# A strided slice by DMA alone: hand-set semaphores in a critical section against waits set by the tile framework

## The chip, the cores and the metric

The kernel runs on one core of one Trainium2 chip. The metric is the device time of one execution in microseconds; the time of a kernel is the median over its runs. The kernel does no arithmetic: every byte is moved by the core's 16 DMA engines, and the only engines of the core that take part are SyncE (SP) and ScalarE (ACT), both merely as issuers of transfers. A "transfer" below is one `dma_start`.

## What is computed

```
batch, seq, dim = 32, 1024, 512          # x is float32
start, stop, stride = 0, 512, 2
def reference(x, start, stop, stride):
    return x[:, start:stop:stride, :].astype(np.float32)
```

The output has 32 batches of 256 rows of 512 float32, so each row is 2 KB, a batch 512 KB and the whole output 16.78 MB. In the input the rows that are taken stand 4 KB apart (every second row of the first half of each batch).

## The kernel before

The 256 rows of a batch are dealt out by parity into two halves of 128 rows. `two(t, b, step, parity)` picks one half of two batches, b and b + step, as 128 x 2 x 512 elements (512 KB); `apart(b)` says which parity of batch b goes which way.

One half of each batch is copied straight from the input to the output in DRAM (line 41): 16 transfers of 512 KB, two batches each, issued by ACT on its own DMA queue (q10 in the profile). They are called the copies here, copy 0 to copy 15.

The other half goes through SBUF. It is loaded into the tile `held` (128 partitions x 32 batches x 512 elements) by 16 transfers of 512 KB, two batches each (line 40, the loads, load 0 to load 15), and stored to the output by 32 transfers of 256 KB, one batch each (line 46, the stores, store 0 to store 31). Loads and stores are both issued by SP on one queue (q1 in the profile), all loads first.

The order is written out by hand inside one critical section (line 33), in which the framework sets no waits. Each group of eight batches has a semaphore `loaded` that its four loads count up by 16 each; SP waits for the full count of a group (line 43) before it issues that group's eight stores. So SP's instruction stream has four waits among its 48 transfers, and ACT's has none among its 16. At the end SP waits for all stores and all copies (lines 47 and 48). Entering and leaving the critical section costs a small handshake between SP and ACT.

An issuer does not wait for a transfer to be done; it goes on as soon as the transfer is handed over. Where an issue takes several us in the profile, the handing over itself was held up.

Of the kernel before, what the change touches and what calls it, by code (L numbers as in the profile page):

```python
# [3 lines left out]

EIGHT = 8


def apart(b):


    return 1 - (b >> 1 & 1)


def two(t, b, step, parity):

    return t[b : b + step + 1 : step].rearrange("b (p two) d -> two p b d", two=2)[parity]


def kernel(tc, x, start, stop, stride, out):

    nc = tc.nc
    src = x[:, start:stop:stride, :]
    B, rows, D = out.shape
    P = rows // 2
    sp, act = nc.sync, nc.scalar
    groups = range(0, B, EIGHT)  # L30
    with tc.tile_pool(name="io", bufs=1) as io:
        held = io.tile([P, B, D], x.dtype, name="held")
        with tc.tile_critical():
            loaded = [nc.alloc_semaphore(name=f"loaded{g}") for g in groups]
            done = [nc.alloc_semaphore(name=f"done{i}") for i in range(2)]
            for g in groups:
                for i, (b, step) in enumerate(((0, 5), (2, 5), (1, 3), (3, 3))):
                    b += g
                    at = g + 2 * i
                    sp.dma_start(held[:, at : at + 2], two(src, at, 1, 1 - apart(at))).then_inc(loaded[g // EIGHT], 16)  # L40
                    act.dma_start(two(out, b, step, apart(b)), two(src, b, step, apart(b))).then_inc(done[1], 16)
            for g in groups:
                sp.wait_ge(loaded[g // EIGHT], 16 * 4)
                for b in range(g, g + EIGHT):
                    to = out[b].rearrange("(p two) d -> two p d", two=2)[1 - apart(b)]
                    sp.dma_start(to, held[:, b]).then_inc(done[0], 16)
            sp.wait_ge(done[0], 16 * B)
            sp.wait_ge(done[1], 16 * (B // 2))


# [1 line left out]
_INS = ['x', 'start', 'stop', 'stride']  # L52
_OUTS = [((32, 256, 512), 'float32')]

_NUMBERS = {'start': 0, 'stop': 512, 'stride': 2}


def kernel(**inputs):
    import numpy as _np
    import concourse.bacc as _bacc  # L60
    import concourse.tile as _tile
    from concourse import mybir as _mybir
    from concourse.bass_utils import run_bass_kernel_spmd as _run

    nc = _bacc.Bacc("TRN2", target_bir_lowering=False, num_devices=1)  # L65
    arrays, args = {}, []
    for name in _INS:
        if name in _NUMBERS:
            args.append(_NUMBERS[name])
            continue  # L70
        a = _np.ascontiguousarray(inputs[name])
        if a.dtype.kind in "iu":
            a = a.astype(_np.int64)
        arrays[f"in_{name}_dram"] = a
        args.append(nc.dram_tensor(f"in_{name}_dram", a.shape, _mybir.dt.from_np(a.dtype), kind="ExternalInput").ap())
    for i, (shape, dtype) in enumerate(_OUTS):
        dt = _mybir.dt.from_np(_np.dtype(dtype))
        args.append(nc.dram_tensor(f"out_{i}_dram", shape, dt, kind="ExternalOutput").ap())
    with _tile.TileContext(nc) as tc:
        kernel(tc, *args)  # L80
    r = _run(nc, [arrays], core_ids=[0])
    got = tuple(r.results[0][f"out_{i}_dram"] for i in range(len(_OUTS)))
    return got[0]
```

## Time and profile before

| | |
|---|---|
| median of 7 runs | 81.12 us (80.43 to 81.68) |
| the profiled execution's own time | 81.0 us |
| its span, first to last instruction | 79.2 us |
| time around the span | 1.8 us |
| loads: issue, duration of one (min / median / max) | 437 / 1556 / 7242 ns |
| copies: the same | 662 / 1863 / 5182 ns |
| stores: the same | 492 / 642 / 4267 ns |
| first issue of a load, first and last issue of a store | 0.9 us, 34.0 us, 67.4 us |

The page has a row for each compute engine that is busy (here only POOL, with four tiny fills of constants at the start), then a digit per fortieth of the span for how busy the 16 DMA engines were, and the rate in GB/s that they moved. A transfer is counted once in the moved bytes, so the 25.17 MB are 8.39 MB of loads, 8.39 MB of copies and 8.39 MB of stores. Issues of transfers are not counted as busy time of an engine; they have a section of their own, with the time from an issue to the landing of its last byte. A DMA share slightly above 1 means that packets of one engine overlap a little in the record.

A landing can also be read from the semaphores: each transfer adds 16, one from each DMA engine, and the time of the sixteenth is its landing. Where many transfers share a semaphore, the records are taken in sixteens in order of time.

### The profile page before, as it was taken

How to read it: one execution, taken by the hardware profiler on the slowest of the kernel's cores; microseconds unless marked ns; L12 is line 12 of the kernel's file. 1: busy time of each engine (PE TensorE's matmuls, PEld its weight loads, DVE VectorE, ACT ScalarE, POOL GpSimd, SP SyncE). 2: the span in 40 equal slices, each digit the busy share in tenths (PEclk: the TensorE clock that was granted, in tenths of full speed). 3: DMA queues.
4: the chain of work that ended last, by engine and by line, in shares of the span. 5: the costliest groups of instructions: out<-in, count | busy, mean ns of one | idle time of the engine just before them, and what ended most of it. 6: DMA issues, size and time to landing. Idle time of an engine off the chain costs nothing. (4 is left out here: it accounts for less than half of the span.)

```text
span 79.2 us, 115 instructions
## 1 busy us (share of the span) xinstructions
POOL 0.2 (0%) x4
## 2 busy tenths in 40 slices
POOL 1000000000000000000000000000000000000000
DMA  0899989999999999999999999999999999999970
GB/s 0 251 310 239 331 281 329 342 344 358 320 341 379 344 337 269 261 332 316 349 344 357 374 279 347 344 291 404 408 404 383 351 342 362 349 360 359 350 260 7
DMA packets 13312, 25.17 MB, mean 318 GB/s; under 512 B 1024, under 2 KB 1024, under 8 KB 13312
## 3 DMA queue, kind: packets, MB, share of 16 engines
q1 hardware_dynamic: 8960, 16.78, 64.9%
q10 hardware_dynamic: 4352, 8.39, 30.6%
HBM read 16.78 MB, written 16.78 MB: 424 GB/s over the span
## 5 line engine op out<-in xcount | busy, mean ns | idle before, releaser
L65 POOL MEMSET const-bfloat16-1.0<- 128x1 bf16 x1 | 0.1, 101 | 0.0
L65 POOL MEMSET const-uint8-127<- 128x1 uint8 x1 | 0.1, 101 | 0.0
L65 POOL MEMSET const-float32-0.0<- 128x1 f32 x1 | 0.1, 98 | 0.2 <-issue 0.2
L65 POOL MEMSET const-float32-1.0<- 128x1 f32 x1 | 0.1, 98 | 0.0
## 6 DMA issues: line engine op xcount, KB each, us to landing
out_dram<-in_x_dram ACTq DMA_DIRECT2D x16, 512.0 KB, 22.3
held<-in_x_dram SPq DMA_DIRECT2D x16, 512.0 KB, 22.4
out_dram<-held SPq DMA_DIRECT2D x32, 256.0 KB, 10.3
```

What stands on the lines that cost most here:

```text
L65: nc = _bacc.Bacc("TRN2", target_bir_lowering=False, num_devices=1)
```

## The change

The critical section, its hand-made semaphores and the waits on them go. `held` becomes 16 tiles, one per load. The same loads, copies and stores are written in the same order on the same two queues, and the tile framework places the waits.

```
-    groups = range(0, B, EIGHT)
     with tc.tile_pool(name="io", bufs=1) as io:
-        held = io.tile([P, B, D], x.dtype, name="held")
-        with tc.tile_critical():
-            loaded = [nc.alloc_semaphore(name=f"loaded{g}") for g in groups]
-            done = [nc.alloc_semaphore(name=f"done{i}") for i in range(2)]
-            for g in groups:
-                for i, (b, step) in enumerate(((0, 5), (2, 5), (1, 3), (3, 3))):
-                    b += g
-                    at = g + 2 * i
-                    sp.dma_start(held[:, at : at + 2], two(src, at, 1, 1 - apart(at))).then_inc(loaded[g // EIGHT], 16)
-                    act.dma_start(two(out, b, step, apart(b)), two(src, b, step, apart(b))).then_inc(done[1], 16)
-            for g in groups:
-                sp.wait_ge(loaded[g // EIGHT], 16 * 4)
-                for b in range(g, g + EIGHT):
-                    to = out[b].rearrange("(p two) d -> two p d", two=2)[1 - apart(b)]
-                    sp.dma_start(to, held[:, b]).then_inc(done[0], 16)
-            sp.wait_ge(done[0], 16 * B)
-            sp.wait_ge(done[1], 16 * (B // 2))
+        held = [io.tile([P, 2, D], x.dtype, name=f"held{i}") for i in range(B // 2)]
+        for g in range(0, B, EIGHT):
+            for i, (b, step) in enumerate(((0, 5), (2, 5), (1, 3), (3, 3))):
+                b += g
+                at = g + 2 * i
+                sp.dma_start(held[at // 2], two(src, at, 1, 1 - apart(at)))
+                act.dma_start(two(out, b, step, apart(b)), two(src, b, step, apart(b)))
+        for b in range(B):
+            to = out[b].rearrange("(p two) d -> two p d", two=2)[1 - apart(b)]
+            sp.dma_start(to, held[b // 2][:, b % 2])
```

In the built program of the changed kernel the framework uses eight DMA semaphores, `DMAHW0` to `DMAHW7`, and deals them out in turn in the order of the program: copies get the even ones, loads the odd ones, and the stores go through all eight. Every transfer waits until the transfer before it on its semaphore has landed in full. A cut of the listing, with the count each waits for:

```
ACT copy 0   ->DMAHW0        SP load 0   ->DMAHW1
ACT copy 1   ->DMAHW2        SP load 1   ->DMAHW3
...
ACT copy 4   waits DMAHW0 16     SP load 4   waits DMAHW1 16
...
ACT copy 15  waits DMAHW6 48     SP load 15  waits DMAHW7 48
SP store 0   waits DMAHW0 64     SP store 1   waits DMAHW1 64
...
SP store 31  waits DMAHW7 112
```

So copy i waits for copy i - 4, load i for load i - 4, stores 0, 2, 4 and 6 for copies 12 to 15, stores 1, 3, 5 and 7 for loads 12 to 15, and store j from 8 on for store j - 8. At the end SP waits for all eight semaphores. The number of transfers and of bytes is the same, and so is the order on each queue.

## Prediction

> **What bounds the kernel now.** I read the page first: does anything but the DMA engines matter, and are these ever idle?
>
> ```profile
> span 79.2 us, 115 instructions
> ...
> DMA  0899989999999999999999999999999999999970
> GB/s 0 251 310 239 331 281 329 342 344 358 320 341 379 344 337 269 261 332 316 349 344 357 374 279 347 344 291 404 408 404 383 351 342 362 349 360 359 350 260 7
> ...
> q1 hardware_dynamic: 8960, 16.78, 64.9%
> q10 hardware_dynamic: 4352, 8.39, 30.6%
> ```
>
> The two queues together fill 64.9 + 30.6 = 95.5% of the 16 engines' time over the whole span. Only the first slice and the last two are not near full. The second view is the same by stages, in stretches that I chose from the semaphore landings: both queues run until about 54.5 us (load 15 lands at 54.5, copy 15 at 55.9), stores alone after that.
>
> ```profile
> core 0: us, POOL busy (x), PEclk, DMA share, GB/s
> 0.00:5.00 5.00, 0.20 (x4) 1.00 0.53 171
> 5.00:10.00 5.00, 0.00 (x0) 1.00 0.97 283
> 10.00:12.00 2.00, 0.00 (x0) 1.00 0.82 282
> 12.00:54.50 42.50, 0.00 (x0) 1.00 1.02 333
> 54.50:59.50 5.00, 0.00 (x0) 1.00 1.05 404
> 60.00:75.00 15.00, 0.00 (x0) 1.00 1.06 355
> 75.00:76.00 1.00, 0.00 (x0) 1.00 0.94 315
> 76.00:77.00 1.00, 0.00 (x0) 1.00 0.70 268
> 77.00:78.00 1.00, 0.00 (x0) 1.00 0.09 35
> ```
>
> The columns are length, POOL, clock, DMA share and rate. The engines are full from about 5 us to 75 us, so an issuer matters only if it leaves a queue empty. The third view says how far the issuers run ahead: time from issue to landing, for loads (L40), copies (L41) and stores (L46).
>
> ```profile
> L40 SPq DMA_DIRECT2D held<-in_x_dram x16: 437/1556/7242, 0.9 to 30.7; - x16
> DMA to landing us min/median/max: 4.1/22.4/27.4
> ...
> L41 ACTq DMA_DIRECT2D out_dram<-in_x_dram x16: 662/1863/5182, 0.9 to 33.6; - x16
> DMA to landing us min/median/max: 6.4/22.3/25.3
> ...
> L46 SPq DMA_DIRECT2D out_dram<-held x32: 492/642/4267, 34.0 to 67.4; - x32
> DMA to landing us min/median/max: 9.2/10.3/21.3
> ```
>
> A load takes 4.1 us when nothing lies ahead of it (load 0) and 22.4 us in the median: the difference is waiting in line. Stores are issued from 34.0 us, yet none lands before 53 us, as SP's queue is served in order and the loads are ahead of them. The last view is the end of SP's chain:
>
> ```profile
> SPq L33 <- DMA out_dram<-held: 10.0, 1, 10.0
> ```
>
> SP issues its last store at 67.4 us and then has 10 us with nothing to do but wait. The DMA engines set the end, not SP.
>
> **The change part by part.** No byte, transfer or queue order changes, so the sum starts from the profiled execution's 81.0 us (0.12 under the median of 81.12; span 79.2 and 1.8 around it). What changes is how many transfers may be in flight.
>
> *Loads and copies: at most 4 per queue.* Before, the limit is the queue itself: the issue of load 9 runs from 8.85 to 16.1 us and ends as load 3 lands (16.2 us by the semaphores), so about 6 are in flight. Now load i waits for load i - 4. Four loads and four copies are 8 x 0.524 = 4.19 MB; at the 324 GB/s of this stage (all of 2.0 to 54.5 us) that is 12.9 us of work. A new transfer needs 4.1 us (load 0) to 6.4 us (copy 0) from issue to landing on near-empty queues. When load i - 4 lands, three loads are still queued, 3 x 3.24 us = 9.7 us of work beside the copies, against at most 6.4 us to bring in the next. The engines do not run in step: the first and the last of a load's sixteen increments lie 1.2 to 3.1 us apart. Even an engine 3.1 us ahead has 9.7 - 3.1 = 6.6 us. Cost 0; the cover is the three queued transfers. Behind the waiting instruction stand all later loads and stores on SP and all later copies on ACT. From below: if the dip at 10 to 12 us (share 0.82) comes from the held-up issues, it goes, a gain of 2 x 0.18 = 0.36 us. From above: losing 3% of the stage, about the difference between shares of 1.02 and 0.99, is 1.6 us. I take 0, nearest to the row of 12 to 54.5 us.
>
> *Turn from loads to stores.* Store 0 now waits for copy 12, which landed at 46.7 us, where before SP issued it at 34.0. Behind it on SP stand the 31 other stores. At 46.7 us, loads 13, 14 and 15 (landing at 47.8, 51.1, 54.5) are still on SP's queue, so it has 7.8 us of its own work left. Store 2 follows copy 13 (50.1 us), store 4 copy 14 (53.4), store 6 copy 15 (55.9). So when loads end at 54.5, stores 0 to 5 are queued: 6 x 0.262 MB / 404 GB/s = 3.9 us. Store 6 enters at 55.9 and store 7 half a us later. Cost 0, with 54.5 + 3.9 - 55.9 = 2.5 us to spare, less what stores 0 to 5 were served earlier in the copies' place (which is no loss, as the engines then worked on them).
>
> *Stores: at most 8 in flight,* where the 10.3 us median and 355 GB/s (0.74 us a store) make about 14 before. Eight are 8 x 0.74 = 5.9 us of work. An unqueued round trip is not in the trace; the nearest row is load 0 with 4.1 us, for twice the bytes and a cold start, so it bounds a store's from above, unless engines that lag add to it. They do: at the end the share falls from 0.94 to 0.09 between 75 and 77.6 us, so the fastest engine ends about 2.4 us before the slowest. For the last engine, whose landing releases the next store, seven are still queued (5.2 us) against 4.1 us. It never runs dry. One that leads may, for 4.1 + 2.4 - 5.9 = 0.6 us, which moves no end. SP keeps up: 0.64 us per issue (median) against 0.74 us drained. Cost 0; bounds: +1.8 us (three rounds of eight that each expose 0.6) and -1.0 us (leading engines held back, so that the late engines end sooner: the idle area of 75 to 77.6 us is 0.12 + 0.36 + 0.97 over 1.06, less the 0.4 us after the last packet).
>
> Here a rule stands against the change. The Trainium skill, "DMA: Bandwidth & Descriptors", section "Anatomy of one DMA — SWDGE (gpsimd) path", says that a transfer has a fixed cost near 2.0 us, mostly the receipt of the last byte, and that engines never wait on semaphores, so a wait holds the issuer and all behind it. Read harshly, an estimate by that page, the 32 stores would go in four rounds of eight, each exposing 2.0 us: 8 us more, 89.0. By the row of load 0 against the window of 5.9 us it is 0, because stores are replaced one by one. No run here shows a waited store yet.
>
> *Entry and exit of the section.* In the trace's records SP's entry signal and its wait stand between the start barrier (0.65 us) and the first load (0.94 us); removing them is worth about 0.1 us. At the end SP's wait is over at 78.11 us and its final barrier begins at 78.59 us. Between them lies the handshake with ACT. In its place come four waits for semaphores and a drain, of which two are left once store 31 has landed, at some 0.07 us each (the spacing of SP's records there). So 0.48 - 0.14 = 0.34 us. Both are on the path: -0.44 us. Bounds 0 and -0.6.
>
> Sum: 81.0 + 0 + 0 + 0 - 0.44 = 80.56, rounded to 80.6 us.
>
> **The rivals.**
> *Slower: the window of eight stores is too short.* It decides once a store's round trip, lag of engines included, is over 5.9 us. For: 4.1 + 2.4 = 6.5 us is over it. Against: those 2.4 us are the lead of the first engines and not a delay of the late ones. Price: 3 x (6.5 - 5.9) = 1.8 us, so 81.0 - 0.44 + 1.8 = 82.4. At 7.0 us it would be 3.3 us, 83.9.
> *Slower: the window of four in the first stage.* For: it is a third less than the queue held. Against: the four loads and three copies issued in the first 3 us landed after 9.8 and 11.3 us in the median, so they alone kept the engines busy to about 12 us. Price: 1.6 us, 82.2.
> *Faster: a shorter line serves better.* Engines kept closer together end together (-1.0), or the dip at 10 to 12 us goes (-0.36). For: the ragged end; in 54.5 to 59.5 us the rate is 404, later 355 GB/s, so engines slow each other. Against: the lag of an engine, 3 stores, is less than the window of 8, so it hardly holds them back. 79.6 with the first alone, 79.2 with both.
> *The change does nothing that shows:* waits placed differently, each covered, and the 0.44 us lost in the spread of 80.43 to 81.68. That gives 81.0.
>
> **How the numbers follow.** Covered waits with the shorter entry and exit, 80.6: 0.40. Nothing at all, 81.0: 0.12. Store window 0.18, first window 0.12, faster 0.18. The range leaves out half of the faster case below 79.5 and the store window's worse part above 82.7, together a good 0.15. A difference of 1% (0.8 us) is about what a measurement of this kernel can tell from none. Against the median the likeliest is -0.55%, so some of its chance (0.08) passes the 1% with the faster case: faster 0.26. The two slower windows less a little that stays inside 1%: slower 0.28. Within 1%: 0.46. Cases of both signs hold a part, so the likeliest one's own range is 80.1 to 81.1.
>
> **What would show it.** Median time to landing falls from 22.4 to some 13 us for loads and from 10.3 to some 6 us for stores. The share stays at 1.0 or more from 12 to 75 us. Issues of loads last about 0.5 to 0.9 us, never 7, and their waits appear on SP and ACT instead. The first store is issued at 46 to 47 us and the last at 71 to 73 us. SP's final wait is 5 to 6 us instead of 10. From the last landing to the end it takes 0.8 us instead of 1.1. The prediction is wrong if the share sags below 1 between 56 and 74 us (store window), between 12 and 54 us (first window), or if packets get quicker at the same share, which nothing here accounts for.

## The result, and the profile after

| | before | after |
|---|---|---|
| median | 80.79 us (59 runs) | 80.23 us (24 runs) |
| ratio | | 0.9936, 95% interval 0.9919 to 0.9953 |
| the profiled execution's own time | 81.0 us | 80.27 us |
| its span | 79.2 us | 78.5 us |

With more runs than the prediction had, the kernel before has a median of 80.79 us. By the ratio the change takes 0.64% off it, 0.52 us (0.38 to 0.65). The forecast was 80.6 us from 81.0, that is 0.44 us less. Executions that took over 1.5% longer than the fastest of the same kernel are left out of all ratios and intervals, and of the times of direct_only and raw_mixed below.

The page of the changed kernel, the same rows as were read of the kernel before:

```profile
span 78.5 us, 109 instructions
...
DMA  0898999997999999999999999999999999999990
GB/s 5 291 281 245 303 317 337 325 349 258 361 371 364 310 370 348 314 341 278 310 384 332 363 329 316 346 266 402 406 405 392 350 348 361 351 355 359 354 307 25
...
q1 hardware_dynamic: 8960, 16.78, 64.8%
q10 hardware_dynamic: 4352, 8.39, 31.8%
```

The DMA engines are as full as before: the same bytes on the same queues, 64.8 + 31.8 = 96.6% of a span that is 0.7 us shorter. By stages (length, POOL, clock, DMA share, rate):

```profile
core 0: us, POOL busy (x), PEclk, DMA share, GB/s
0.00:5.00 5.00, 0.20 (x4) 1.00 0.58 178
5.00:10.00 5.00, 0.00 (x0) 1.00 0.88 276
10.00:12.00 2.00, 0.00 (x0) 1.00 0.98 327
12.00:54.50 42.50, 0.00 (x0) 1.00 1.02 334
54.50:59.50 5.00, 0.00 (x0) 1.00 1.05 406
60.00:75.00 15.00, 0.00 (x0) 1.00 1.06 355
75.00:76.00 1.00, 0.00 (x0) 1.00 0.96 324
76.00:77.00 1.00, 0.00 (x0) 1.00 0.46 170
```

From 12 to 75 us share and rate are those of before to within 2 GB/s (333, 404 and 355 then). The whole stage of loads and copies, 2 to 54.5 us, moved 326 GB/s against 324. The dip of 10 to 12 us is gone, but there is one at 5 to 10 us instead. What did change is the length of the lines: time from issue to landing of loads, copies and stores in the changed kernel, and how long one issue takes (ns, min/median/max):

```profile
L36 SPq DMA_DIRECT2D held<-in_x_dram x16: 367/368/844, 0.7 to 41.0; - x16
DMA to landing us min/median/max: 4.2/12.6/14.5
...
L37 ACTq DMA_DIRECT2D out_dram<-in_x_dram x16: 580/580/904, 0.7 to 43.5; - x16
DMA to landing us min/median/max: 6.2/12.6/14.6
...
L40 SPq DMA_DIRECT2D out_dram<-held x32: 332/608/767, 46.4 to 72.2; - x32
DMA to landing us min/median/max: 3.8/5.6/9.1
```

The median load lands after 12.6 us instead of 22.4, the median store after 5.6 instead of 10.3. No issue is held up for several us any more: a load's issue took up to 7242 ns and now at most 844. That time is now spent in waits, which SP's waits show (waiter, what it waited for, us in total, times, longest):

```profile
SPq L36 <- DMA held<-in_x_dram: 33.7, 12, 4.1
SPq L40 <- DMA out_dram<-in_x_dram: 11.5, 4, 5.0
SPq L71 <- DMA out_dram<-held: 5.0, 4, 3.4
SPq L40 <- DMA out_dram<-held: 1.5, 5, 0.4
```

These are 46.7 us of new waits ahead of transfers, and yet the engines are full. Where the 0.7 us of span went is seen at its ends:

```profile
0.73 43.31 ACTq L37 DMA_DIRECT2D out_dram<-in_x_dram  x16
0.73 40.65 SPq L36 DMA_DIRECT2D held<-in_x_dram  x16
46.39 26.14 SPq L40 DMA_DIRECT2D out_dram<-held  x32
```

The first load is issued at 0.73 us instead of 0.94. At the end, from the last landing in the semaphore records to the end of the span, it takes 0.79 us (77.69 to 78.48) instead of 1.16 (78.06 to 79.22). Together 0.20 + 0.37 = 0.57 us. Between first issue and last landing lie 76.96 us against 77.16, a difference of 0.2 us, which is less than this stretch differs from profile to profile (76.35 to 77.65 in crit_windows, raw_no_tile, before_sections4, crit_stores4, raw_short and raw_long_again below, which keep the order of the transfers).

### The profile page after: what moved, and what is told of

Read it like the earlier page. It is cut to its first block, busy times and chain, and to the rows that moved or that the text cites. A ratio compares the mean times of both kernels' runs of the same rounds, so it can differ in the third digit from the quotient of the medians.

```text
span 78.5 us, 109 instructions
## 1 busy us (share of the span) xinstructions
POOL 0.2 (0%) x4
## 3 DMA queue, kind: packets, MB, share of 16 engines
q1 hardware_dynamic: 8960, 16.78, 64.8%
q10 hardware_dynamic: 4352, 8.39, 31.8%
HBM read 16.78 MB, written 16.78 MB: 428 GB/s over the span
## 6 DMA issues: line engine op xcount, KB each, us to landing
out_dram<-in_x_dram ACTq DMA_DIRECT2D x16, 512.0 KB, 12.6
held<-in_x_dram SPq DMA_DIRECT2D x16, 512.0 KB, 12.6
```

## Experiments

Theory A: the gain is the handshakes of the critical section at both ends, and the shorter lines are free because what is still queued covers each wait. Theory B: a shorter line serves better, and the handshakes are hidden. Theory C: the waits cost something, and a larger gain at the ends pays for it. All kernels below write the whole output. The code is cut to the lines that matter, and some of them are shortened.

**crit_windows: the waits alone.**

```
 with tc.tile_critical():
+    # a semaphore for each of 4 loads, 4 copies and 8 stores
     ...
+    if n >= 4: sp.wait_ge(lane[n % 4], 16 * (n // 4))
     sp.dma_start(held[:, at : at + 2], ...).then_inc(lane[n % 4], 16)
+    if n >= 4: act.wait_ge(copied[n % 4], 16 * (n // 4))
     act.dma_start(...).then_inc(copied[n % 4], 16)
     ...
+    if b < 8:  sp.wait_ge((copied, lane)[b % 2][b // 2], 64)
+    if b >= 8: sp.wait_ge(stored[b % 8], 16 * (b // 8))
     sp.dma_start(to, held[:, b]).then_inc(stored[b % 8], 16)
```

> The critical section stays, with its entry and exit, but every transfer waits as in the changed kernel (loads and copies for the one four earlier, stores 0 to 7 for copies and loads 12 to 15, later stores for the one eight earlier). Theory A (the gain is the handshakes at both ends, the shorter lines are free): as before, 80.8 us, ratio 0.998 to 1.002. Theory B (the gain is the shorter line, which serves better, and the handshakes are hidden): as the changed kernel, 80.2 us, ratio 0.992 to 0.995. Theory C (the shorter line costs something that a larger gain at the ends paid for): over 81.0 us, ratio 1.003 or more.

Measured: 80.32 us, before 80.35; ratio 1.0004 (0.9981 to 1.0027). The lines are as short as in the changed kernel, and the first load is issued where it was before; the section on DMA issues (KB each, median us to landing) and the order of time:

```profile
out_dram<-in_x_dram ACTq DMA_DIRECT2D x16, 512.0 KB, 12.4
held<-in_x_dram SPq DMA_DIRECT2D x16, 512.0 KB, 12.0
out_dram<-held SPq DMA_DIRECT2D x32, 256.0 KB, 5.3
```

```profile
0.91 43.37 ACTq L47 DMA_DIRECT2D out_dram<-in_x_dram  x16
0.94 40.40 SPq L44 DMA_DIRECT2D held<-in_x_dram  x16
```

The waits by themselves are worth nothing within 0.2 us either way. Theory B's 0.992 to 0.995 lies outside the interval, C's 1.003 just outside. A stands. The traces of this chip agree: from first issue to last landing it takes 76.37 and 76.43 us with short lines (crit_windows, crit_stores4) and 76.63 and 76.35 us with long ones (raw_no_tile, before_sections4).

**raw_no_tile: the ends alone.**

```
-with tc.tile_pool(name="io", bufs=1) as io:
-    held = io.tile([P, B, D], x.dtype, name="held")
-    with tc.tile_critical():
+held = nc.alloc_sbuf_tensor("held", [P, B, D], x.dtype).ap()
     ...
-with _tile.TileContext(nc) as tc:
-    tile_strided_slice_kernel(tc, *args)
+tile_strided_slice_kernel(nc, *args)
```

> The kernel before with its own four waits and its long lines, but without the critical section and also without the framework's closing barriers. Theory A: 0.2 us less at the entry; at the exit the 1.1 us from the last landing to the end of the span shrink to about 0.1 us, so 1.2 us less in all, 79.6 us, ratio 0.985. Theory B: the line is as long as before, so no gain from it; at most the closing barriers (0.6 us) go, 80.2 us or more, ratio 0.993 to 1.0.

Measured: 78.91 us, ratio 0.9834 (0.9791 to 0.9876). The order of time and the section on DMA issues:

```profile
0.73 33.45 SPq L37 DMA_DIRECT2D held<-in_x_dram  x16
```

```profile
held<-in_x_dram SPq DMA_DIRECT2D x16, 512.0 KB, 21.9
```

Loads land after 21.9 us in the median, so the lines are long. The first load is issued at 0.73 us, and from the last landing to the end there are 0.04 us instead of 1.16. That is 0.20 + 1.12 = 1.32 us of the span. The time around the span is shorter too, 78.77 - 77.4 = 1.4 us instead of 1.8, so 1.7 us go at the ends in all. By the ratio it is 0.0166 x 80.35 = 1.33 us (1.0 to 1.7), and for the same code on another chip (raw_long_again below) 0.0211 x 81.22 = 1.71 us. Within the noise, what goes at the ends goes from the time, one for one.

**before_sections4: the suspected cost, more often.**

```
 with tc.tile_pool(name="io", bufs=1) as io:
     held = io.tile([P, B, D], x.dtype, name="held")
+    for _ in range(4):
+        with tc.tile_critical():
+            sp.nop()
+            act.nop()
     with tc.tile_critical():
```

> The kernel before with four more critical sections ahead of its own, each holding one empty instruction on SP and one on ACT, so that four more entries and exits lie ahead of the first transfer. Theory A: each costs what its entry (0.21 us) and exit (0.35 us) cost at the ends, 4 x 0.55 = 2.2 us more, 83.0 us (82.6 to 83.6), ratio 1.027. Theory B: they are hidden, 80.8 us, ratio 1.00.

Measured: 82.99 us, ratio 1.0338 (1.0306 to 1.0371), 2.7 us more. In order of time:

```profile
3.22 34.88 ACTq L45 DMA_DIRECT2D out_dram<-in_x_dram  x16
3.25 32.50 SPq L44 DMA_DIRECT2D held<-in_x_dram  x16
```

The first load starts 3.25 - 0.94 = 2.31 us later, 0.58 us for each section, where 0.55 was expected. The handshakes are not hidden. The ratio's 2.5 to 3.0 us is somewhat more than these 2.3; where the rest lies is open. That the time itself met the forecast of 83.0 us is luck: the kernel before took 80.35 us on this chip, not the 80.8 that the forecast started from.

**crit_stores4, crit_stores2: how much cover the store window has.** As crit_windows, with four or two stores in flight and no store waiting for a copy.

```
-    if b < 8:  sp.wait_ge((copied, lane)[b % 2][b // 2], 64)
-    if b >= 8: sp.wait_ge(stored[b % 8], 16 * (b // 8))
+    if b % 2 == 0: sp.wait_ge(lane[b // 2 % 4], 16 * (b // 8 + 1))
+    if b >= 4: sp.wait_ge(stored[b % 4], 16 * (b // 4))     # or 2
```

> The kernel before with loads and copies limited to four in flight and stores to four instead of eight; no store waits for a copy. Theory A with a window that must cover a store's round trip: four stores are 4 x 0.74 = 2.95 us of work, the shortest store in the changed kernel's trace takes 3.8 us from issue to landing, so each of 7 rounds of four exposes at least 0.85 us: 6 us more, 86.8 us; with the lag between engines (2.4 us) added to the round trip up to 92 us. Rival (the memory sets the pace of stores at 355 GB/s and the depth of the line does not matter): 80.8 us.

Measured: 80.08 us, ratio 0.9981 (0.9958 to 1.0005). My number for the round trip was wrong. The stores of that run:

```profile
L55 SPq DMA_DIRECT2D out_dram<-held x32: 332/332/709, 42.0 to 74.7; - x32
DMA to landing us min/median/max: 2.3/2.9/13.5
```

The shortest store of the changed kernel (3.8 us) had still waited in line, by 1.5 us or more. Even here the median of 2.9 us is about the work of the four stores in flight (2.95 us), so it can hold time in line too, and the next run had two.

> As the run with four stores in flight, but with two. There a store took 2.9 us from issue to landing in the median and 2.3 us at the least, and four of them (2.95 us of work) just covered it. Two are 1.48 us of work. Theory A2 (a window must cover the round trip of a store that has nothing ahead of it, and that is 2.3 us, not the 3.8 to 4.1 us that I took): a store every 2.3/2 = 1.15 us instead of 0.74, 32 x 0.41 = 13 us more, 93.5 us (90 to 96). Rival (even two keep the memory busy): 80.4 us.

Measured: 91.02 us, ratio 1.1313 (1.1255 to 1.1372). Its page and its stores:

```profile
DMA  0899999999999999999999994666666666666661
GB/s 5 290 278 292 327 273 299 387 379 342 358 372 341 327 267 346 285 366 361 361 350 323 334 343 173 236 236 245 257 253 248 251 239 250 252 251 253 250 242 74
```

```profile
L55 SPq DMA_DIRECT2D out_dram<-held x32: 332/332/591, 41.7 to 85.5; - x32
DMA to landing us min/median/max: 2.1/2.1/13.2
```

This is what a window that is too short looks like: the digits fall to 6 for the whole stage, and 250 GB/s are two stores (0.524 MB) in 2.1 us. A store takes 2.1 us there whether the store before it was issued some 0.6 or 1.5 us earlier, so it does not wait in line, and 2.1 us is its round trip. (In crit_turn_last below, store 0 meets empty queues and takes 2.2 us.) Theory A2 holds with that number, and the time lies in its 90 to 96 us: the window of eight, 5.9 us of work, covers the round trip almost three times.

**crit_loads2: the first window.** As crit_stores4 with two loads, two copies and eight stores in flight.

> The critical section with two loads and two copies in flight instead of four and four; eight stores. Theory A by the rows of the prediction: a pair of transfers needs 4.2 to 6.2 us from issue to landing and engines lie 1.2 to 3.1 us apart, so a round trip near 7.5 us against 6.5 us of work in the window: each of 16 pairs takes 3.75 us instead of 3.24, 8 us more, 88.4 us (84 to 92). Theory A2 (round trips on a short line are shorter than these rows, as with the stores): within 1% of 80.4 us.

Measured: 84.53 us, ratio 1.0503 (1.0438 to 1.0568), at the lower edge of theory A's range: 0.0503 x 80.56 = 4.1 us more where its sum had 8. Copies and loads by the section on DMA issues, and the stretch from 12 to 54.5 us:

```profile
out_dram<-in_x_dram ACTq DMA_DIRECT2D x16, 512.0 KB, 7.4
held<-in_x_dram SPq DMA_DIRECT2D x16, 512.0 KB, 6.7
```

```profile
12.00:54.50 42.50, 0.00 (x0) 1.00 0.99 312
```

A load's landing takes 6.7 us in the median there, a copy's 7.4, against 6.5 us of work in the window. The rate is 312 GB/s where it was 333. So four in flight cover the wait and two do not; three were not tried.

**crit_turn_last: the turn from loads to stores.** As crit_stores4 with eight stores in flight, but store 0 waits for all copies:

```
+    if b == 0:
+        for k in range(4): sp.wait_ge(copied[k], 64)
```

> The critical section with windows of four, four and eight, and store 0 waits for the last copy (about 55.9 us) instead of copy 12 (46.4 us), so SP's queue holds no store when the last load lands. Theory A (the prediction's cover of 2.5 us at the turn is real and its loss is paid in full): the last engines run dry from about 55.5 us until store 0 arrives, some 0.4 us of wait and issue and 1 us to its first packet, so 1.6 us more (1.2 to 2.6), 82.0 us, ratio 1.020. Rival (the stores' stage goes at the memory's 355 GB/s after a first stretch at 405, so a gap at its start is made up by a longer quick stretch): less than 0.5 us more, ratio under 1.006.

Measured: 82.06 us, ratio 1.0193 (1.0144 to 1.0242), theory A's 1.020. The page and SP's longest wait for a copy:

```profile
DMA  0898899999999899899999999945999999999980
GB/s 0 268 290 262 281 340 328 351 331 376 361 323 367 296 288 366 300 333 322 369 342 368 284 342 375 321 163 209 383 377 387 378 358 358 356 356 364 353 294 3
```

```profile
SPq L52 <- DMA out_dram<-in_x_dram: 12.8, 1, 12.8
```

The first store is issued at 54.3 us instead of 46.4, and the two digits 4 and 5, from 52 to 56 us, are the hole. Part of it is made up, as the rival said: from 60 to 75 us the rate is 364 GB/s instead of 355. In the changed kernel the same place has digits of 9: the waits for copies 12 to 15, one by one, keep the queue fed. One more dependence here costs 1.9% (1.4 to 2.4).

**direct_only: can the bound be moved?** Built as the changed kernel, without SBUF:

```
-sp.dma_start(held[at // 2], two(src, at, 1, 1 - apart(at)))
+sp.dma_start(two(out, b, step, 1 - apart(b)), two(src, b, step, 1 - apart(b)))
 act.dma_start(two(out, b, step, apart(b)), two(src, b, step, apart(b)))
-for b in range(B): ...
```

> Built in the manner of the changed kernel, but both halves of every batch go from DRAM to DRAM, 16 copies on each of the two queues, none through SBUF: 8.39 MB fewer pass the DMA engines (8192 packets of 2 KB instead of 12288), while DRAM is read and written as before. Theory A (the DMA engines' packets are the bound, 95 to 97 ns each): 8192/16 x 0.096 = 49 us and 4 us at the ends, 53 us. Rival (DRAM traffic is the bound: in the first stage 326 GB/s moved are 163 of loads and 163 of copies, so 326 read and 163 written, 489 GB/s): 33.55 MB / 489 GB/s = 68.6 us and 4 us, 72.6 us.

Measured: 82.66 us (82.62 and 82.70), ratio 1.0271 (1.0202 to 1.034). Neither was right.

```profile
12.00:54.50 42.50, 0.00 (x0) 1.00 0.94 218
60.00:75.00 15.00, 0.00 (x0) 1.00 0.96 219
```

The engines are nearly full but move 218 GB/s: a third fewer packets of 2 KB, each longer (142 and 137 ns in the mean on the two queues, against 98 and 97 in the changed kernel). A full DMA share is thus no proof that the engines themselves are the bound.

**raw_short, raw_mixed, raw_stores_act, raw_long_again: is there a version that beats both?** All without critical section and closing barriers. The first has four loads, four copies and four stores in flight, the second issues each pair of stores after the load four places on, the third gives the stores to ACT.

```
 raw_mixed:        for i in range(4, 16): load(sp, i); store(sp, i - 4)
 raw_stores_act:   for i in range(16): load(sp, i); copy(sp, i // 2) if i % 2
                   for i in range(16): store(act, i)
                   for i in range(8, 16): copy(sp, i)
```

> As the run without critical section and closing barriers, but with four loads, four copies and four stores in flight. Theory A (the lines' length is free down to these windows; what the ends cost is independent of it): as that run with its long lines, ratio 0.983 (0.980 to 0.987). Rival (a short line gives 0.2% by itself, as the run with four stores hinted, 0.9981 with an interval that reached 1.0005): 0.981 or less, 0.4 us under the other with several runs.

Measured: 79.23 us, ratio 0.9724 (0.9698 to 0.9749). That is below theory A's range and within the rival's "0.981 or less", but further down than the 0.2% that the rival gave to a short line.

> As the run without critical section, but SP issues the stores of a pair of batches after the load four places on, so that loads and stores alternate on its queue, beside ACT's copies and after them. Theory A (the stages stay full whatever the order; the sum of packets sets the time): as without, 79.2 us, ratio 0.983. Rival (stores alone are paced by the memory's writes at 355 GB/s, while mixed with loads the engines go at up to 404): the 8.39 MB of the last stage take 20.8 us instead of 23.6, 2 to 3 us less, 76.5 us, ratio 0.95.

Measured: 82.68 us, ratio 1.0103 (1.0039 to 1.0166). Neither was right. The copies are done at 59.1 us, and from 60 to 75 us, with loads and stores alone on one queue, the rate is 335 GB/s where stores alone had 355; from 12 to 54.5 us it is 322 instead of 333. So the mix did not go faster, which the rival needed; why is open.

> As the run without critical section, but ACT issues the stores from the first load on, and SP issues loads and copies, two loads to a copy and then the last eight copies. Theory A: the order is free, ratio 0.983 or so. Rival (a mix with reads all the time is better than writes alone at the end): 76 to 77 us, ratio 0.95. Against both: DRAM to DRAM copies alone moved 219 GB/s, so if the last eight copies (4.19 MB) run without loads beside them they take 19 us instead of 13 at 326 GB/s, 85 us.

Measured: 85.92 us, ratio 1.0562 (1.0503 to 1.0621), near the 85 us of the warning in its last sentence, but not for its reason. The last eight copies take from 68 to 84 us, and until 77.6 us stores run beside them. After that copies run alone, on one queue, and the page has these slices of 2.1 us for it (the last two full ones, 78.0 to 82.2 us):

```profile
DMA  0998899999989999999999999999999999999992
GB/s 6 315 274 264 272 399 404 272 353 318 267 259 390 359 252 211 307 405 368 248 346 344 252 244 322 403 332 211 347 367 253 216 330 384 301 274 297 318 352 101
```

Copies alone moved 318 and 352 GB/s there, with packets of 97 ns, and not the 219 of direct_only. So 219 GB/s is no bound on copies from DRAM to DRAM as such. In direct_only two queues copied at once, and both halves of the same batches; which of these made its packets longer no run shows. Why raw_stores_act is slower is open as well.

> The kernel without critical section and closing barriers, with its long lines, once more, because its ratio (0.9834) and that of its twin with short lines (0.9724) were measured on two chips, on which the kernel before had 80.35 and 81.44 us. Theory A (the lines' length is free, the difference is the chips): the ratio follows the chip's own time of before, near 79.0 us for this kernel and anywhere from 0.972 to 0.985. Rival (short lines gain 1%): 0.983 again, whatever before takes on this chip.

Measured: 79.56 us, ratio 0.9789 (0.9742 to 0.9835), on a third chip with 81.22 us for the kernel before. The same code thus has 0.9834 and 0.9789, and the intervals of raw_long_again and raw_short overlap slightly. Whether short lines add a little of their own, up to some 0.5 us, stays open; in crit_windows they added nothing within 0.2 us. The three runs without section and barriers that keep the order (raw_no_tile, raw_short, raw_long_again) are 1.7 to 2.8% faster than the kernel before. None ran beside the changed kernel; its 0.64% taken off, 1.0 to 2.1% are left.

## Why the prediction was right

*The start of the sum.* The time came out 0.33 us under the 80.56 of the sum, and 0.21 of this is the start: 81.0 was one execution, and the median of 59 is 80.79. The -0.55% that the prediction gives against the median is 0.44 over that 81.0; against the median of 81.12 the sum is -0.69%.

*The bound.* Right in what the sum uses: from 12 to 75 us the share stayed at 1.02 to 1.06 and the rates within 2 GB/s. That the full share makes the engines themselves the limit is not shown; in direct_only the share is nearly as full with packets over 40% longer.

*Loads and copies, four per queue: taken at 0.* Right: 326 against 324 GB/s. The predicted landing of 13 us was 12.6. crit_windows puts the whole of the waits at 0.0 ± 0.2 us, and crit_loads2 shows that the cover was what made them free: with half the window the wait cost 4.1 us. The gain of 0.36 us that I allowed for the dip at 10 to 12 us did not come; a dip moved to 5 to 10 us.

*The turn: taken at 0.* Right. The first store went out at 46.4 us (46 to 47 was forecast) and crit_turn_last made the cover visible by removing it.

*Stores, eight in flight: taken at 0.* The value was right, the term under it was mis-sized. The round trip of a store alone was bounded by 4.1 us from a load of twice the size; it is 2.1 us. The rival that added the engines' lag of 2.4 us and came to 6.5 us was therefore far off: half the window still cost nothing. Nor is the lag a fixed time to be added: from the first to the last of a store's sixteen increments it takes 1.3 to 2.2 us in the changed kernel, 0.5 to 0.9 with four in flight and 0.2 to 0.3 with two (from the first store that waits for another), and with eight in crit_turn_last, where the stores meet empty queues, 0.2 to 1.0. The harsh reading of the Trainium skill, "DMA: Bandwidth & Descriptors", section "Anatomy of one DMA — SWDGE (gpsimd) path", would have made it 89.0 us. The page's fit itself, 2.0 us and the bytes over 436 GB/s, gives 2.6 us for 256 KB as an estimate, nearer to the measured 2.1 than my row was, although the page fits it to transfers issued by GpSimd and these are issued by SP. Four in flight hid the round trip and two did not.

*Entry and exit: -0.44 us.* Right in sign and place, a little small: 0.20 us at the entry where 0.1 was taken, 0.37 at the exit where 0.34 was. Their sum, 0.57 us, agrees with the measured 0.52 (0.38 to 0.65).

*The faster rival.* A shorter line did not serve better: crit_windows has the short lines and gains nothing. That engines slow each other, which the rival read from 404 and then 355 GB/s, no run shows; the fall is in both kernels (404 and 406, then 355).

*The signs.* SP's last wait was 5.0 us (5 to 6 forecast), the last store went out at 72.2 us (71 to 73), from last landing to end it took 0.79 us (0.8; before, it was 1.16, a little more than the 1.1 that the prediction read). An issue of a load took 0.37 us at the least, where I had 0.5.

## What to carry to other kernels

Ask of a wait how much is still queued for the engines when it ends, in us of work, and set it against the round trip of one transfer that has nothing ahead of it; a median to landing from a full queue says nothing about that round trip. Where the DMA engines are full from end to end and transfers and order are to stay, what is left to gain is the time before the first issue and after the last landing; here it counted one for one within the noise, so look there for handshakes. Find the margin by shrinking the window until the DMA digits fall, not by estimating it.

## What the runs showed that was not expected

A store of 256 KB that does not wait in line lands 2.1 us after the start of its issue. From 54.5 to 59.5 us, where all but the end of the last copy is stores, the rate is 404 to 406 GB/s, and from 60 to 75 us it is 355, in both kernels. With both queues copying from DRAM to DRAM, the core moved 218 GB/s at a share of 0.94 to 0.96, so that half of the output taken through SBUF, where its bytes are moved twice, was the shorter way: 80.6 against 82.7 us on the same chip. Yet copies alone on one queue moved 318 and 352 GB/s at the end of raw_stores_act in a stretch of 4 us; whether one queue of copies could keep that up was not tried (16.78 MB at 335 GB/s would be 50 us, an estimate). The kernel before had medians of 80.35 to 81.44 us on the chips of these runs, more than the change is worth; only runs on the same chip could be compared.
